# A two-layer encoder on one core: a weight sum made by an accumulating DMA instead of VectorE, with its subtraction moved one product later, and an operand difference made in two parts

## The chip, the cores and the metric

The kernel runs on one core of a Trainium2 chip. A core has TensorE (PE, matrix products; PEld is its loading of weights), VectorE (DVE), ScalarE (ACT), GpSimd (POOL) and SyncE (SP). SP issues the plain loads; GpSimd issues the transfers that add to what lies at their destination. The metric is the device time of one execution in microseconds.

## The reference

The reference is an encoder trunk in float32 with 528 tokens (512 and 16 learned ones), width 1024, two layers. Each layer is a half feed-forward network (FFN), a mixer, and a second half FFN:

```python
def swiglu(x, w_gate, w_up, w_down):
    return (jax.nn.silu(x @ w_gate) * (x @ w_up)) @ w_down

for l in range(DEPTH):
    h = h + 0.5 * swiglu(rmsnorm(h, norm_gains[l, 0]),
                         ffn_w_gate[l, 0], ffn_w_up[l, 0], ffn_w_down[l, 0])
    h = h + mixer(rmsnorm(h, norm_gains[l, 1]), w_in[l], ...)
    h = h + 0.5 * swiglu(rmsnorm(h, norm_gains[l, 2]),
                         ffn_w_gate[l, 1], ffn_w_up[l, 1], ffn_w_down[l, 1])
return rmsnorm(h, final_norm)[:, N_META:]
```

The mixer (gated linear attention beside softmax attention) is not touched by the change. The inner width of an FFN is 2816, that is 22 tiles of 128 columns.

## The kernel before

**Split weights.** Every float32 product is made of three matmuls in the faster type fp32r. `Weights.make` splits each weight block of 128 x 1024 (512 KB) into a high half `whi` (a copy by ScalarE, L287) and a low half `wlo` (block minus high half, VectorE, L288). It works up to four blocks ahead of TensorE's use (`AHEAD_MADE`, one less inside an FFN), and `Weights.fetch` has SP load blocks up to nine ahead. Pools of 3 raw blocks, 4 high and 4 low halves and 3 + 3 sums (tags `wsa`, `wsb`) set when a buffer comes free.

**Seven products in place of eight.** The gate and up projections take their columns in 11 pairs of tiles per FFN. A pair's block product is done by a Winograd scheme with seven products, named by the characters "1" to "7". "1", "2" and "4" use the loaded blocks 11, 12 and 22 as they are. The four others need sums of blocks, for pairs 2 to 10:

- "7" uses s3 = block 21 - block 11. Block 21 is loaded into its buffer (`begin_sums`), and VectorE subtracts in place (L244).
- "6" uses s2 = block 22 + s3, added in place by VectorE (L253).
- "3" uses s4 = s2 - block 12 (VectorE, L256).
- "5" uses s1 = block 21 + block 22: a load, and then an accumulating DMA (`first_sum`, `Weights.add`, L208) which GpSimd issues.

`sums` is called by `make` behind the low half of "1", "2" and "6". Pairs 0 and 1 of each FFN, and the weights of the down-projection, make their sums in other ways, which the change leaves alone.

**Groups.** The 11 pairs form groups of 4, 4 and 3. Behind each of the first two, a fast down-projection follows, again with seven products: an "O" step makes its operands in high and low halves from the four hidden tiles of a quarter (first three of the four, later the last one), and "S" steps run its products on the two halves of the output. The operand "6" is the difference of two quarters (`difference`, L674), then a high half by ScalarE (L669) and a low half by VectorE (L670). In the order of a group's end, `ffn_steps` puts the first products of the next group's first pair (pairs 4 and 8) between the last "S" steps:

```python
turns = [("S", g, *t, 3) for t in zip(AB, "16273465734")]
steps += turns[:6]
for s, c in zip(turns[6:], "1265"):
    steps += [s, ("P", p + 1, c)]
steps.append(turns[-1])
```

So at pairs 4 and 8 there is one "S" step of 24 matmuls between products "2" and "6". At the other pairs "7", "4" and "3" lie in between, of the pair itself or of the one before.

**The order of work.** Each engine runs its instructions in the order in which the program issues them. TensorE writes its sums into PSUM; ScalarE and VectorE take them out (L598 copies a snapshot, L604 adds to it; L716 adds a result of the down-projection to h). ScalarE's copies of weights (L287) and VectorE's low halves (L288) stand in line with these.

Of the kernel before, what the change touches and what calls it, by code (L numbers as in the profile page):

```python
# [14 lines left out]
ALU = mybir.AluOpType  # L15
# [155 lines left out]
class Weights:  # L171
# [59 lines left out]
    def sums(self, f, i, product, w):  # L231


        got, V = self.summed, self.nc.vector
        if (f, i) in OPENING and product in "12":
            (self.begin_sums if product == "1" else self.first_sum)(f, i, *[w] * (product == "1"))
        if i < 2:
            if product == "2":
                s4 = self.negative(f, i, "s4", w)
                self.add(s4, got[f, i, "6"])  # L240
                got[f, i, "3"] = s4
        elif product == "1":
            if i < NPAIR:
                V.tensor_tensor(got[f, i, "7"], got[f, i, "7"], w, ALU.subtract)  # L244
            else:
                got[f, i, "7"] = self.negative(f, i, "s3", w)
                self.add(got[f, i, "7"], self.dram(f, i, "21"))
            if not i < NPAIR:
                self.add(got[f, i, "6"], got[f, i, "7"])
        elif product == "2":  # L250
            self.kept = w
            if i < NPAIR:
                V.tensor_tensor(got[f, i, "6"], got[f, i, "6"], got[f, i, "7"], ALU.add)  # L253
        elif product == "6":
            s4 = self.long.tile([P, SLAB], F32, tag="wsa", name=f"s4_{f[0]}{f[1]}_{i}")
            V.tensor_tensor(s4, w, self.kept, ALU.subtract)  # L256
            got[f, i, "3"] = s4
# [42 lines left out]
    def next(self, name):  # L300
        t = PLAN[self.pos]
        assert t[1] == name, (t, name)
        s, c = divmod(COLUMN[self.pos], SLAB)
        self.pos += 1
        hi, lo = self.use(self.at[s])
        return hi[:, c : c + t[5]], lo[:, c : c + t[5]]
# [18 lines left out]
def build(tc, ctx, xt, wts, win, par, w2, const, umask, out):  # L325
    nc = tc.nc
    V, S, G, TE = nc.vector, nc.scalar, nc.gpsimd, nc.tensor
# [24 lines left out]
    def close_pools(pools):  # L352
        for n in reversed(pools):
            slots.pop(n).release()
# [28 lines left out]
    def h(c, cs=None):  # L383
        return hall[:, c, cs or slice(0, live[0])]
# [184 lines left out]
    def ffn(l, f, norm, done, following):  # L569

        x, rs, up, n = norm.x, None, None, live[0]
        w = n // 2
        pools = open_pools("left", psum=("s2",), c=4, s2=2)
        made, hid, sums, raw, sets = {}, {}, {}, {}, {}
        risen = iter(range(KC))

# [81 lines left out]
        def operand(g, c, ks=slice(0, 4)):  # L658

            src = raw[g][{"1": 0, "2": 2, "5": 0, "6": 0, "7": 1, "3": 3, "4": 2}[c]]  # L660
            if (g, c) not in sets:
                tag = "c" if c in "56" else "g"
                sets[g, c] = [quarter(tag, F32R) for _ in range(2)]
            hi, lo = [t[:, ks] for t in sets[g, c]]
            if c == "3":
                S.activation(hi, src[:, ks], AF.Copy, scale=-1.0)
                V.scalar_tensor_tensor(lo, src[:, ks], -1.0, hi.bitcast(F32), ALU.mult, ALU.subtract)
            else:
                S.copy(hi, src[:, ks])  # L669
                V.tensor_tensor(lo, src[:, ks], hi.bitcast(F32), ALU.subtract)  # L670

        def difference(g, into, a, b, ks=slice(0, 4)):
            r = raw[g]
            V.tensor_tensor(r[into][:, ks], r[a][:, ks], r[b][:, ks], ALU.subtract)  # L674

        def operands_of(g, ks, order):
            for c in order:
                if c == "5":
                    difference(g, 0, 1, 0, ks)
                operand(g, c, ks)  # L680
# [10 lines left out]
        def fast_down(g, dq, c, part):  # L691
            last = sum(GROUPS[: g + 1]) - 1
            kinds = ("ss", "s2") if last % 2 == 0 else ("s2", "ss")
            st = made.setdefault(("S", g, dq), {})
            where = {"2": "Y", "5": "Z", "3": "Z"}.get(c, "X")
            begin = c in "125"
            if part != 2:
                if begin:
                    st[where] = pair(kinds[{"Y": 0, "Z": 1, "X": dq}[where]] == "s2")
                st["w"] = st.get("w", {})  # L700
                st["w"][c] = W.op((l, f), NPAIR + QUADS * g + dq, c, ahead=AHEAD_MADE - 1)
            acc = st[where][:, :, :w]
            hi, lo = st["w"][c]
            xs = sets[g, c]
            for k in {1: range(3), 2: range(3, 4), 3: range(4)}[part]:
                for j in range(2):
                    for i, (a, b) in enumerate(((hi, 0), (hi, 1), (lo, 0))):
                        TE.matmul(acc[:, j], a[:, j, k], xs[b][:, k], start=bool(begin and k == 0 and i == 0),  # L708
                                  stop=k == 3 and i == 2, skip_group_check=not begin)
            if part == 1:  # L710
                return
            st["w"].pop(c)
            for m, q in {"1": [(0, 0)], "2": [(0, 0)], "5": [(1, 1)], "6": [(0, 1)], "3": [(0, 1)], "7": [(1, 1)],
                         "4": [(1, 0)]}[c]:
                to = hall[:, 4 * dq + m : 4 * dq + m + 3 : 2, q * w : (q + 1) * w]
                V.tensor_tensor(to, to, acc, ALU.add)  # L716
            if dq == 1:
                sets.pop((g, c))
            operands_behind(g, dq, c)

        def down(g, m, first, last):
            base = 2 * sum(GROUPS[:g])
            other = (sum(GROUPS[: g + 1]) - 1) % 2 == 0
            kind = "s2" if other == (m // 2 % 2 == 1) else "ss"
            width = 2 * GROUPS[g]
            if g == len(GROUPS) - 1 and m >= LATE and done is None:
                sums[m] = Acc("ss" if m == LATE else "s2", cut=True), [W.next("ffn_w_down") for _ in range(width)]
                if m == KC - 1:
                    ending([sums[c] for c in range(LATE, KC)], [hid[base + k] for k in range(width)], rs)
                return  # L730
            if first == 0:
                sums[m] = Acc(kind)
            product("ffn_w_down", sums[m], [hid[base + k] for k in range(first, last)], last - first,
                    begin=first == 0, end=last == width)
            if last < width:
                return
            add_to_h(m, sums[m])
            if g == len(GROUPS) - 1:
                lower_h(m, rs)
                (done or finish_chunk)(m)  # L740
# [3 lines left out]
        for i, step in enumerate(steps):  # L744
            if step[0] == "P":
                if step[1:] == (0, "5") and norm.acc is None:
                    for c in range(KC):
                        norm.square(c)
                product_of_pair(*step[1:])
                if step[1:] == (0, "5"):  # L750
                    rs, up = norm.rs(True)
                    W.behind = prev_act[0]
                if step[1] in (2, 3) and step[2] in "6574":
                    m = next(risen)
                    V.scalar_tensor_tensor(h(m), h(m), -1.0, up, ALU.mult, ALU.mult)
                if i == last_op:
                    close_pools(norm.pools)
                    following()
            elif step[0] == "S":
                fast_down(*step[1:])  # L760
            elif step[0] == "O":
                g, last = step[1:]
                operands_of(g, slice(3, 4) if last else slice(0, 3), "215" if last else "125")
                if last:
                    difference(g, 0, 3, 0)
                    operand(g, "6")
            else:
                down(*step[1:])
# [444 lines left out]
    def finish_chunk(c):  # L1213
        fin.square(c)
        gain(c, slice(0, SEQ))

    def ending(sums, operand, rs):

        table("abs_reciprocal_sqrt_and_small")
# [64 lines left out]
    for l in range(DEPTH):  # L1284
        a, b, c = norms[3 * l : 3 * l + 3]
        ffn(l, 0, a, b.chunk, lambda: operand_pools(b, "x"))
        close_pools(bp.pop())
        mixer(l, b, c.chunk_of_pair, lambda: (operand_pools(c, "xc"), bp.append(block_pools())))
        if l < DEPTH - 1:
            d = norms[3 * l + 3]  # L1290
            ffn(l, 1, c, d.pair_of, lambda: operand_pools(d, "xc"))
        else:
            ffn(l, 1, c, None, lambda: None)
# [72 lines left out]
```

## Time and profile before

| | before |
|---|---|
| median of 3 runs | 2219.3 us (2217.36 to 2219.31) |
| profiled execution | 2218.53 us |
| its span | 2216.8 us |
| granted TensorE clock | 0.998 |
| TensorE busy | 2164.6 us (98%) |
| VectorE busy | 1784.4 us (80%) |
| ScalarE busy | 1210.7 us (55%) |
| GpSimd busy | 101.5 us (5%) |
| queue of GpSimd's DMAs (q0) | 60.82 MB, 15.6% of the 16 DMA engines' span |
| queue of SP's DMAs (q1) | 245.53 MB, 33.0% |

The times come from one execution that the hardware profiler recorded. In the lines of its views `out<-in` names the tiles without their numbers: `whi<-w` is the high half of a loaded or summed weight block, `wlo<-w,whi` its low half, `s` a sum, `g` and `c` operands and hidden tiles, `ss` a PSUM sum. A timeline line has the start, the duration, the engine, the source line and the operation; in brackets stands the idle time before it and what ended it. A wait line has the engine and line that waited, what for, the total in us, how many times and the longest. A DMA line has the issues, the size of each and the median from issue to landing.

### The profile page before, as it was taken

The numbers are of one execution on the slowest core, as the hardware profiler recorded it, in microseconds if no ns is written. First come the engines' busy times: TensorE is split into PE (matmuls) and PEld (weight loads), VectorE is DVE, ScalarE is ACT, GpSimd is POOL, SyncE is SP. The second block draws the span as 40 slices with busy tenths as digits, with TensorE's granted clock in tenths as the row PEclk, the third lists the DMA queues.
The fourth block names the chain that finished last, engine by engine and source line by source line (L and its number), as shares of the span: only waits on it lengthen the run. The fifth ranks groups of instructions, "written<-read, shape, count | busy, mean of one in ns | idle before, by whom it ended". The sixth has DMA issues, their size and how long they took to land.

```text
span 2216.8 us, 40090 instructions
## 1 busy us (share of the span) xinstructions
PE 2164.6 (98%) x16506; PEld 2070.7 (93%) x16506; DVE 1784.4 (80%) x2695; ACT 1210.7 (55%) x1779; POOL 101.5 (5%) x120
## 2 busy tenths in 40 slices
PE   7999999999999999999999999999999999999998
PEld 6899999989999999999999999999788888999997
DVE  7887978486886688888789879775879767997987
ACT  7444545354785555454575445553557836554543
POOL 1000000000000001000010000000000001000100
PEclk9999999999999999999999999999999999999999
DMA  9675753212113467666566757432121146776752
GB/s 278 172 199 165 190 158 101 86 48 67 48 39 118 116 168 200 190 184 187 158 162 187 207 159 194 143 110 77 48 82 53 42 135 153 196 200 180 191 161 67
DMA packets 87463, 311.41 MB, mean 140 GB/s; under 512 B 9712, under 2 KB 12144, under 8 KB 87280
## 3 DMA queue, kind: packets, MB, share of 16 engines
q1 hardware_dynamic: 68624, 245.53, 33.0%
q0 software_dynamic: 16704, 60.82, 15.6%
q8 instruction: 130, 2.13, 0.4%
q10 hardware_dynamic: 1952, 2.50, 0.3%
q14 instruction: 53, 0.43, 0.1%
HBM read 289.94 MB, written 2.10 MB: 132 GB/s over the span
## 4 chain that ended last, share of the span: by engine, by line
PE 79%; DVE 11%; ACT 3%; issue 2%; DMA 1%; DVEq 0%; POOL 0%; ACTq 0%; POOLq 0%
PE ss L594 36%; PE mm L461 13%; PE ss L708 11%; PE ss L461 10%; PE sm L461 2%; DVE wlo L288 2%; DVE g L674 1%; PE sm L1069 1%; PE ss L1044 1%; DVE h L716 1%; PE ss L467 1%; DMA w<-win 1%; PE sm L1085 1%; ACT t L440 1%; DVE c L670 1%
## 5 line engine op out<-in xcount | busy, mean ns | idle before, releaser
L594 PE MATMUL ss<-xc,whi 128*128 128x264 f32 (+1 forms) x4928 | 905.3, 285 | 15.6 <-ACT whi L287 7.6
L594 PEld LDWEIGHTS ss<-xc,whi 128*128 128x128 f32 x4928 | 765.3, 189 | 20.5 <-ACT c L598 8.4
L594 PE MATMUL ss<-xc,wlo 128*128 128x264 f32 (+1 forms) x2464 | 701.5, 285 | 8.8 <-DVE wlo L288 8.7
L594 PEld LDWEIGHTS ss<-xc,wlo 128*128 128x128 f32 x2464 | 465.4, 189 | 11.2 <-DVE wlo L288 11.0
L288 DVE TENSOR_TENSOR wlo<-w,whi 128x1024 fp32r<-128x1024 f32 (+1 forms) x337 | 408.0, 1217 | 64.1 <-ACT whi L287 63.9
L287 ACT CAST whi<-w 128x1024 fp32r<-128x1024 f32 (+1 forms) x337 | 349.4, 1048 | 175.2 <-PE ss L594 82.1
L461 PE MATMUL mm<-x,whi 128*128 128x264 f32 (+1 forms) x1712 | 384.8, 315 | 0.0
L461 PEld LDWEIGHTS mm<-x,whi 128*128 128x128 f32 x1712 | 278.4, 188 | 16.6 <-issue 1.0
L461 PE MATMUL mm<-x,wlo 128*128 128x264 f32 (+1 forms) x856 | 266.0, 315 | 0.0
L708 PE MATMUL ss<-g,whi 128*128 128x264 f32 (+1 forms) x1280 | 238.6, 285 | 1.5 <-ACT g L669 1.4
L287 ACT CAST whi<-raw 128x1024 fp32r<-128x1024 f32 x126 | 132.1, 1048 | 163.6 <-PE mm L461 102.8
L598 ACT COPY c<-ss 128x528 f32<-128x528 f32 (+1 forms) x132 | 78.4, 594 | 259.1 <-PE ss L594 259.1
L288 DVE TENSOR_TENSOR wlo<-raw,whi 128x1024 fp32r<-128x1024 f32 x126 | 153.9, 1221 | 59.2 <-ACT whi L287 58.4
L708 PEld LDWEIGHTS ss<-g,whi 128*128 128x128 f32 x1280 | 199.0, 189 | 2.1 <-ACT g L669 1.6
L708 PE MATMUL ss<-g,wlo 128*128 128x264 f32 (+1 forms) x640 | 181.7, 284 | 0.0
L461 PEld LDWEIGHTS mm<-x,wlo 128*128 128x128 f32 x856 | 159.5, 188 | 8.5 <-issue 0.7
L461 PE MATMUL ss<-g,whi 128*128 128x264 f32 (+2 forms) x900 | 166.2, 299 | 0.0
L461 PEld LDWEIGHTS ss<-g,whi 128*128 128x128 f32 x900 | 131.7, 188 | 5.3
L208 POOL DMA_DIRECT2D w<-win x60 | 52.8, 880 | 1580.1 <-DVE wlo L288 463.9
L708 PEld LDWEIGHTS ss<-g,wlo 128*128 128x128 f32 x640 | 120.9, 189 | 0.0
L440 ACT ACTIVATE c<-c 128x528 f32<-128x528 f32 (+1 forms) x88 | 56.5, 642 | 93.6 <-DVE c L638 89.3
L708 PE MATMUL ss<-c,whi 128*128 128x264 f32 (+1 forms) x512 | 100.3, 289 | 7.1 <-DVE c L670 6.6
(267 smaller groups left out, 3375.3 us busy)
## 6 DMA issues: line engine op xcount, KB each, us to landing
w<-win SPq DMA_DIRECT2D x335, 512.0 KB, 4.5
raw<-wts SPq DMA_DIRECT2D x126, 512.0 KB, 3.3
w<-win POOLq DMA_DIRECT2D x60, 512.0 KB, 7.5
s<-win POOLq DMA_DIRECT2D x24, 512.0 KB, 7.0
w<-s POOLq DMA_DIRECT2D x24, 512.0 KB, 5.6
s<-w POOLq DMA_DIRECT2D x8, 512.0 KB, 7.7
h<-xt SPq DMA_DIRECT2D x3, 528.0 KB, 7.1
out<-h ACTq DMA_DIRECT2D x4, 256.0 KB, 2.4
```

The source lines that it names most:

```text
L208: self.nc.gpsimd.dma_start(t, src, accum_op=ALU.add)
L287: nc.scalar.copy(hi[:, cs], w[:, cs])
L288: nc.vector.tensor_tensor(lo[:, cs], w[:, cs], hi[:, cs].bitcast(F32), ALU.subtract)
L440: prev_act[0] = S.activation(*args, **kw).ins
L461: TE.matmul(acc.half[i][:width], lhs, rhs[:, acc.spans[i]], start=first, stop=last)
L467: TE.matmul(a, weights, x[:, hs], start=True, stop=True)
L594: TE.matmul(acc[:, j], a[:, j, k], b[:, at], start=bool(begin and k == 0 and i == 0), stop=k == len(x) - 1 and i == 2, skip_group_check=no ...
L598: W.behind = S.copy(part(st, q), acc).ins
L670: V.tensor_tensor(lo, src[:, ks], hi.bitcast(F32), ALU.subtract)
L674: V.tensor_tensor(r[into][:, ks], r[a][:, ks], r[b][:, ks], ALU.subtract)
L708: TE.matmul(acc[:, j], a[:, j, k], xs[b][:, k], start=bool(begin and k == 0 and i == 0), stop=k == 3 and i == 2, skip_group_check=not begin)
L716: V.tensor_tensor(to, to, acc, ALU.add)
```

## The change

It has two parts. In `sums` the subtraction for s3 is no longer done at product "1": the raw block is kept, and VectorE subtracts it at product "2", where it added s2 before. s2 is then made by an accumulating DMA from s3's buffer to s2's, issued by GpSimd. It concerns nine pairs in each of four FFNs, 36 sums. At pairs 4 and 8 this DMA is issued behind the one of `first_sum` of the same pair.

In `ffn` the difference for operand "6" is done in both "O" steps, three quarters of the columns in the first and one quarter in the last, rather than whole in the last. There are eight such sites, two in each FFN.

```diff
@@ -241,7 +241,7 @@
         elif product == "1":
             if i < NPAIR:
-                V.tensor_tensor(got[f, i, "7"], got[f, i, "7"], w, ALU.subtract)
+                self.kept1 = w
             else:
@@ -250,7 +250,8 @@
         elif product == "2":
             self.kept = w
             if i < NPAIR:
-                V.tensor_tensor(got[f, i, "6"], got[f, i, "6"], got[f, i, "7"], ALU.add)
+                V.tensor_tensor(got[f, i, "7"], got[f, i, "7"], self.kept1, ALU.subtract)
+                self.add(got[f, i, "6"], got[f, i, "7"])
@@ -760,9 +761,10 @@
             elif step[0] == "O":
                 g, last = step[1:]
-                operands_of(g, slice(3, 4) if last else slice(0, 3), "215" if last else "125")
+                ks = slice(3, 4) if last else slice(0, 3)
+                operands_of(g, ks, "215" if last else "125")
+                difference(g, 0, 3, 0, ks)
                 if last:
-                    difference(g, 0, 3, 0)
                     operand(g, "6")
```

In the changed order of VectorE's instructions the subtraction of the pairs 4 and 8 stands where the addition L253 stood; at the other pairs it keeps its place.

## The prediction

> **What bounds the kernel now.** I began with the page: the busy table, then the chain that ended last.
>
> ```profile
> span 2216.8 us, 40090 instructions
> PE 2164.6 (98%) x16506; PEld 2070.7 (93%) x16506; DVE 1784.4 (80%) x2695; ACT 1210.7 (55%) x1779; POOL 101.5 (5%) x120
> PE 79%; DVE 11%; ACT 3%; issue 2%; DMA 1%; DVEq 0%; POOL 0%; ACTq 0%; POOLq 0%
> ```
>
> TensorE is busy for 2164.6 of 2216.8 us. All that is not matmul is 52 us, so the change can only move time by closing a pause of TensorE or by opening one. VectorE is 80% busy; work taken from it counts only where TensorE waits for it. So I read next the waits of TensorE.
>
> ```profile
> PE ss L594 <- DVE wlo L288: 8.7, 8, 3.1
> PE ss L594 <- ACT whi L287: 7.6, 2, 7.4
> PE ss L708 <- DVE c L670: 6.6, 8, 0.9
> PE ss L594 <- ACT c L598: 6.1, 11, 0.7
> ```
>
> The third line is the one the change aims at: eight waits, 6.6 us, all for the low half of operand "6" of the fast down-projection, which is made behind the difference. No line names the weight sum L253 or the difference L674 directly, and the two lines on the weight halves have ten waits together. TensorE thus seldom waits for weights, and a weight sum that comes too late would show as a new wait.
>
> **Part 1: the early difference (a gain).** One site, from the timelines of VectorE, ScalarE and TensorE at the end of group 1 of the first FFN:
>
> ```profile
> 249.48 1.25 DVE L674 TENSOR_TENSOR g<-g,g 128x1056 f32<-128x1056 f32 x1
> 250.65 1.31 DVE L716 TENSOR_TENSOR h<-h,ss 128x528 f32<-128x528 f32 x2
> 251.93 1.26 DVE L670 TENSOR_TENSOR c<-g,c 128x1056 fp32r<-128x1056 f32 x1
> 250.82 1.07 ACT L669 CAST c<-g 128x1056 fp32r<-128x1056 f32 x1 [1.03 <-DVE g L674]
> 253.24 0.39 PE L708 MATMUL ss<-c,whi 128*128 128x264 f32 x1 [0.91 <-DVE c L670]
> ```
>
> The chain is difference 1.25, ScalarE's copy 1.07, the low half 1.26, and TensorE pauses 0.91 us for it. The change does three quarters of that difference at the first "O" step, so here a piece of 128x264 remains. The pieces that are in the trace already give its time:
>
> ```profile
> 244.37 0.77 DVE L648 TENSOR_TENSOR g<-c 128x264 f32<-128x264 f32 x2
> 245.27 0.43 DVE L670 TENSOR_TENSOR g<-g,g 128x264 fp32r<-128x264 f32 x1
> L674 DVE TENSOR_TENSOR g<-g,g 128x792 f32<-128x792 f32 x6 | 5.9, 983 | 0.2
> ```
>
> 0.43 for 1.25 takes 0.82 us from the chain. ScalarE stood idle for 1.03 us before its copy, so the copy moves up by all of the 0.82. VectorE has two additions, L716, between; if what they add is ready earlier they move up too and the low half starts 0.8 us earlier; if not, the low half stays where it is and nothing is won. So the bounds are 0 and 0.82 per site, and in all no more than the 6.6 us of the wait row. The two additions start without a pause before them, so I take nearly all of it: seven sites of 0.75 and about 0.3 for the shorter first one, 5.5 us.
>
> What the early part adds: eight differences of 128x792 (0.98 us each by the row above) in the first "O" step, ahead of the low halves of the next weights. Those are made about four products ahead of TensorE; I take 0. Were that cover gone it would cost up to 8 x 0.98 = 7.8 us, but the 10 waits for weights above say that it is not gone anywhere but at the start.
>
> **Part 2: the removed additions.** Seen from the source lines:
>
> ```profile
> L253 DVE TENSOR_TENSOR w<-w,w x36: 1217/1220/1227, 55.6 to 2127.1; 128x1024 f32<-128x1024 f32 x36
> L244 DVE TENSOR_TENSOR w<-w,w x36: 1215/1222/1227, 49.2 to 2125.8; 128x1024 f32<-128x1024 f32 x36
>   DMA w<-win: 33.4, 16
> ```
>
> 36 x 1.22 = 44 us of VectorE vanish, and 36 subtractions go from product "1" to product "2". No wait of TensorE hangs on either, so I take 0; the most that it could give is the 8.7 us of waits for low weight halves. VectorE's idle 33.4 us before L244 belongs to VectorE alone and is not a gain. Keeping the raw block of "1" one product longer holds one of three buffers longer; the loads run several products ahead, so 0 as well.
>
> **Part 3: the accumulating DMA (the cost).** Sum "6" is no longer an addition of 1.22 us but a subtraction, an issue by GpSimd and a transfer to wait for. For the other pairs the halves of "6" are made long after the sum; at pair 9 of the first FFN (VectorE's and ScalarE's timelines) they come 17 us later, more than any transfer below needs:
>
> ```profile
> 284.07 1.22 DVE L253 TENSOR_TENSOR w<-w,w 128x1024 f32<-128x1024 f32 x1
> 301.44 1.05 ACT L287 CAST whi<-w 128x1024 fp32r<-128x1024 f32 x1
> ```
>
> It is tight for the first pairs of groups 1 and 2, pairs 4 and 8, eight sites in all: there product "6" follows "2" with a single step of the down-projection between. Pair 8 of the first FFN, from the timelines:
>
> ```profile
> 269.08 1.22 DVE L244 TENSOR_TENSOR w<-w,w 128x1024 f32<-128x1024 f32 x1
> 271.37 0.88 POOL L208 DMA_DIRECT2D w<-win  x1 [24.81 <-DVE h L716]
> 273.72 1.22 DVE L253 TENSOR_TENSOR w<-w,w 128x1024 f32<-128x1024 f32 x1
> 275.14 1.05 ACT L287 CAST whi<-w 128x1024 fp32r<-128x1024 f32 x1
> 276.42 1.22 DVE L288 TENSOR_TENSOR wlo<-w,whi 128x1024 fp32r<-128x1024 f32 x1
> 282.24 0.40 PE L594 MATMUL ss<-xc,whi 128*128 128x264 f32 x2
> 282.48 0.28 PE L594 MATMUL ss<-xc,wlo 128*128 128x264 f32 x1
> ```
>
> Before, "6" has its halves at 276.2 and 277.6, six and five microseconds ahead of TensorE. In the changed kernel the subtraction stands in L253's place. L244 ahead of it is gone, so it ends between 273.8 (all behind L244 moves up) and 274.9 (nothing moves); I take 273.9 and the issue at 274.0. That is 2.6 us behind the issue of first_sum's transfer at 271.37, on the same queue. With 1.05 for ScalarE, 1.22 for VectorE and about 0.1 between, the low half is ready 2.4 us after landing, so TensorE pauses by whatever the landing exceeds 282.48 - 2.4 = 280.1, a latency of 6.1 us.
>
> What such a transfer takes the trace shows in groups only. First the medians of GpSimd's queue, then three single ones:
>
> ```profile
> w<-win POOLq DMA_DIRECT2D x60, 512.0 KB, 7.5
> w<-s POOLq DMA_DIRECT2D x24, 512.0 KB, 5.6
> s<-w POOLq DMA_DIRECT2D x8, 512.0 KB, 7.7
> ```
>
> ```profile
> 771.47 0.86 POOL L208 DMA_DIRECT2D s<-win  x1 [3.44 <-ACT s L203]
> 773.54 0.89 POOL L208 DMA_DIRECT2D s<-w  x1 [1.20 <-ACT t L505]
> 978.65 0.86 POOL L208 DMA_DIRECT2D w<-win  x1 [3.27 <-DVE g L648]
> 982.51 0.87 POOL L208 DMA_DIRECT2D w<-s  x1 [3.00 <-DMA s<-win]
> ```
>
> The DMA view of the window at 773 us gives the second of these a landing after 7.2 us (2.07 behind its forerunner), that at 982 us gives the fourth 4.7 us (3.86 behind):
>
> ```profile
> s<-w POOLq DMA_DIRECT2D x1, 512.0 KB, 7.2
> w<-s POOLq DMA_DIRECT2D x1, 512.0 KB, 4.7
> ```
>
> So the closer behind another accumulation, the longer. The new one is 2.6 behind, nearer to the 7.2 us; and the DMA engines are loaded at this place, as the windows table shows (the last two columns are DMA share and GB/s):
>
> ```profile
> 275.30:279.00 3.70, 3.70 (x33) 3.70 (x32) 3.70 (x4) 1.95 (x2) 0.00 (x0) 1.00 0.95 248
> ```
>
> From 275.3 to 279.0, the very time in which the transfer would run, they are 95% busy. I take 7.2: landing 281.2, a pause of 1.1 us. At 4.7 or 5.6 there is none; at 7.7 from the late issue (275.0) it is 2.6.
>
> One site is tighter, pair 4 of the last FFN:
>
> ```profile
> 1981.30 1.22 DVE L253 TENSOR_TENSOR w<-w,w 128x1024 f32<-128x1024 f32 x1
> 1989.37 0.40 PE L594 MATMUL ss<-xc,whi 128*128 128x256 f32 x2
> 1989.60 0.28 PE L594 MATMUL ss<-xc,wlo 128*128 128x256 f32 x1
> ```
>
> Issue at about 1982.6, landing by 1989.8, low half 1992.2: a pause of 2.6 us. The eight sites together cost 7 x 1.1 + 2.6 = 10.3 us; I add about 1 us for the start of the first FFN, where weights already come late (the wait of up to 3.1 us above). Bounds: 0, and 7 x 2.6 + 3.1 = 21 us.
>
> Queued behind the waiting ScalarE and VectorE instructions are the next weight copy, an addition L716 and the low half of the next down-projection weight. They become some 5 us late, to about 284 us, and TensorE wants them after product "6", from 285.2 on; I count nothing more. On GpSimd nothing of weight stands behind the new issue, 0.87 us each.
>
> The Trainium skill, page "DMA: Bandwidth & Descriptors", section "Anatomy of one DMA — SWDGE (gpsimd) path", states for a transfer that GpSimd issues a fixed part of about 2 us plus the bytes over 436 GB/s. For 512 KB that is an estimate of 3.2 us, with which all eight pauses would vanish and the sum would be the gain alone. The trace disagrees: its medians for this size are 5.6 to 7.7 us, so I go by the rows.
>
> **Sum.** -5.5 + 10.3 + 1 = +5.8 us. The profiled execution took 2218.53 us with its span of 2216.8, so it would come to 2224.3; the median of the runs, 2219.3, lies 0.8 above it, so 2225 us.
>
> **The rivals.** Forecast: the transfer queues behind first_sum's and TensorE pauses some 1.3 us at eight places, 2225 us; chance 0.55.
>
> (a) The transfer lands in 4.5 to 6 us, as the w<-s group's median of 5.6 says (it too is a sum in SBUF). No site pauses, only the early difference counts: 2219.3 - 5.5 = 2214, with the full 6.6 us 2212.7. It decides below 6.1 us from issue to landing. For it: that median. Against: most of those have no forerunner within 3 us, and the 95% above. Chance 0.14. The estimate from the Trainium skill's page above leads to this rival too.
>
> (b) Gain and cost cancel: with 6.8 us the pause is 0.7 at seven sites and 2.2 at the eighth, 7.1 us against 5.5, or the gain is the smaller part and the pauses are few. Between 2215 and 2223; chance 0.21. That the change does nothing at all lies here too, at 2219.
>
> (c) Heavier queueing: the two transfers share the loaded engines, each slows the other and SP's loads. With 7.7 from the late issue it is 21 - 5.5 = +15.5, 2235. Chance 0.10.
>
> **How the numbers follow.** What a measurement of this kernel can tell from no change is about 0.2%, 4.4 us. Faster by more than that is (a) alone where it keeps most of the gain: 0.13. Within it: (b) and a remainder of (a): 0.22. Slower: the forecast and (c): 0.65. The range 2213 to 2235 takes in (a) at its likely end and (c); what is left out is one in ten at either side.
>
> **What would show it.** In the changed kernel's profile: TensorE's wait row L708 <- DVE L670 falls from 6.6 to about 1 us; L594 <- L288 (or L287) grows by 8 to 12 us with waits at pairs 4 and 8 alone; the issues table has 36 transfers w<-w on GpSimd's queue; those at pairs 4 and 8 take 7 us or more. VectorE's busy time falls by some 44 us. I am wrong if those transfers take under 6.1 us (then faster), or if L708's wait stays, or if TensorE waits at the other pairs as well.

## The result, and the profile after

The changed kernel takes 2271.1 us (median of 5 runs, 2266.83 to 2272.49) against 2219.31 us; the ratio is 1.0227, 95% interval 1.0216 to 1.0239. It is 52 us slower. Forecast were 6 us slower and at most 16: the sign was right, the size was not, and the time lies far outside the range.

The page of the changed kernel, the span, the busy times, the software queue's line and the chain:

```profile
span 2269.2 us, 40136 instructions
PE 2181.6 (96%) x16506; PEld 2083.7 (92%) x16506; DVE 1742.4 (77%) x2667; ACT 1211.9 (53%) x1779; POOL 133.5 (6%) x156
q0 software_dynamic: 21888, 79.70, 19.8%
PE 66%; DVE 16%; DMA 9%; ACT 5%; issue 4%; POOL 0%; SPq 0%; DVEq 0%; POOLq 0%; ACTq 0%
```

Two numbers grew by amounts that add to the loss. Time without a matmul went from 52.2 to 87.6 us, that is 35.4 more. But TensorE's busy time grew as well, by 17.0 us for the same 16506 matmuls: they ran slower. VectorE is 42 us less busy, as foreseen, and nothing was gained by it. DMA is now 9% of the chain instead of 1%.

TensorE's waits, the lines that answer to the four of before:

```profile
PE ss L595 <- ACT whi L288: 31.8, 9, 7.5
PE ss L595 <- DVE wlo L289: 23.5, 26, 3.5
PE ss L595 <- ACT c L599: 6.1, 11, 0.7
PE ss L709 <- DVE c L671: 4.0, 9, 0.7
```

The waits for high weight halves grew by 24.2 us, those for low halves by 14.8; the wait for operand "6" fell by 2.6. Together +36.4, which is about all of the idle time that was added.

Pair 8 of the first FFN, from the timelines of GpSimd, VectorE, ScalarE and TensorE:

```profile
276.76 0.86 POOL L208 DMA_DIRECT2D w<-win  x1 [25.31 <-DVE h L717]
279.27 0.89 POOL L208 DMA_DIRECT2D w<-w  x1 [1.65 <-DVE w L253]
277.64 1.22 DVE L253 TENSOR_TENSOR w<-w,w 128x1024 f32<-128x1024 f32 x1
288.76 1.04 ACT L288 CAST whi<-w 128x1024 fp32r<-128x1024 f32 x1 [8.63 <-DMA w<-w]
289.83 1.23 DVE L289 TENSOR_TENSOR wlo<-w,whi 128x1024 fp32r<-128x1024 f32 x1 [7.66 <-ACT whi L288]
289.85 0.51 PE L595 MATMUL ss<-xc,whi 128*128 128x264 f32 x2 [2.58 <-ACT whi L288]
291.11 0.43 PE L595 MATMUL ss<-xc,wlo 128*128 128x264 f32 x1 [0.75 <-DVE wlo L289]
```

The DMA view gives the new transfer 9.4 us from issue to landing:

```profile
w<-w POOLq DMA_DIRECT2D x1, 512.0 KB, 9.4
```

The order of events is the one foreseen: subtraction, issue 2.5 us behind first_sum's, landing, high half, low half, a pause of 2.58 + 0.75 us. At the eight sites the latency was 8.9 to 11.3 us and the pause 2.8 to 5.2 us, 30.4 us in all.

Now the windows of the same place. A line has start:end, the length, the busy times of TensorE, its weight loads, VectorE, ScalarE and GpSimd with the number of instructions, then granted clock, DMA share and GB/s:

```profile
284.00:287.00 3.00, 3.00 (x27) 3.00 (x26) 0.00 (x0) 0.00 (x0) 0.00 (x0) 1.00 1.05 255
287.00:290.00 3.00, 0.42 (x4) 0.21 (x3) 0.17 (x1) 1.24 (x2) 0.00 (x0) 1.00 0.29 107
290.00:293.00 3.00, 2.25 (x11) 2.04 (x12) 3.00 (x4) 1.70 (x2) 0.00 (x0) 0.72 0.00 0
293.00:296.00 3.00, 3.00 (x20) 3.00 (x19) 3.00 (x4) 0.37 (x1) 0.00 (x0) 0.71 0.34 89
296.00:299.00 3.00, 3.00 (x27) 3.00 (x26) 2.62 (x3) 2.69 (x4) 1.51 (x2) 1.00 0.91 300
```

Behind the pause the granted clock falls, and in the window from 293 to 296, where TensorE has no gap, it does 20 matmuls instead of 27. That is the busy time that grew. By the clock's records half speed followed seven of the eight pauses, for 3.4 or 6.8 us each and 30.6 us in all; the shortest pause, 2.77 us at pair 4 of the second FFN, is the one without it. One more stretch of 6.8 us lies in the start of the first FFN, behind a pause of 3.55 us; the kernel before has a single stretch of 3.4 us, at 120.8 us (each without the very end of the program). Half of 30.6 + 6.8 - 3.4 us is the 17.0 us.

The last two columns show a second thing: DMA goes from 1.05 to 0.00 between 290 and 293 us and is back at 0.91 from 296 on. SP's loads had stopped, and then bunched. The waits of SP's queue between 284 and 294 us say what for:

```profile
SPq L198 <- DVE wlo L289: 9.8, 1, 9.8
SPq L198 <- DMA w<-win: 2.4, 1, 2.4
```

A landing held it for 2.4 us, but then it stood 9.8 us for a raw block that VectorE still had to read for a low half; and VectorE, which works in order, was standing at the late low half of product "6". At the eight sites this wait is 9.3 to 11.7 us; before it was 4.2 to 5.4 us at the same places.

What a bunch can do is seen one pair later, at pairs 5 and 6 of the second FFN (VectorE's and TensorE's timelines, and the DMA view for the load issued at 934.38):

```profile
944.99 1.22 DVE L253 TENSOR_TENSOR w<-w,w 128x1024 f32<-128x1024 f32 x1 [7.89 <-DMA w<-win]
946.14 1.22 DVE L289 TENSOR_TENSOR wlo<-w,whi 128x1024 fp32r<-128x1024 f32 x1
947.41 0.39 PE L595 MATMUL ss<-xc,wlo 128*128 128x264 f32 x1 [1.99 <-DVE wlo L289]
w<-win SPq DMA_DIRECT2D x1, 512.0 KB, 10.5
```

A load of SP (median 4.5 us before) takes 10.5 us. The subtraction waits for it 7.89 us, and the low half of another block, ready to be made, stands behind the subtraction on VectorE. In all, VectorE's idle time ahead of these subtractions grew from 33.4 us (before) to 87.1 us:

```profile
  DMA w<-win: 87.1, 17
```

### The profile page after: what moved, and what is told of

It is laid out like the page before. It is cut to its first block, busy times and chain, and to the rows that moved or that the text cites. A ratio compares the mean times of both kernels' runs of the same rounds, so it can differ in the third digit from the quotient of the medians.

```text
span 2269.2 us, 40136 instructions
## 1 busy us (share of the span) xinstructions
PE 2181.6 (96%) x16506; PEld 2083.7 (92%) x16506; DVE 1742.4 (77%) x2667; ACT 1211.9 (53%) x1779; POOL 133.5 (6%) x156
## 3 DMA queue, kind: packets, MB, share of 16 engines
q1 hardware_dynamic: 68624, 245.53, 32.3%
## 4 chain that ended last, share of the span: by engine, by line
PE 66%; DVE 16%; DMA 9%; ACT 5%; issue 4%; POOL 0%; SPq 0%; DVEq 0%; POOLq 0%; ACTq 0%
PE ss L595 29%; PE mm L462 12%; PE ss L462 10%; PE ss L709 6%; DMA w<-win 6%; DVE wlo L289 5%; DMA w<-w 3%; PE sm L462 2%; ACT whi L288 2%; PE sm L1071 1%; DVE g L675 1%; PE ss L1046 1%; DVE g L671 1%; DVE h L717 1%; PE ss L468 1%
## 5 line engine op out<-in xcount | busy, mean ns | idle before, releaser
L595 PE MATMUL ss<-xc,whi 128*128 128x264 f32 (+1 forms) x4928 | 918.5, 287 | 40.6 <-ACT whi L288 31.8
L595 PEld LDWEIGHTS ss<-xc,whi 128*128 128x128 f32 x4928 | 775.6, 191 | 47.2 <-ACT whi L288 34.9
L595 PE MATMUL ss<-xc,wlo 128*128 128x264 f32 (+1 forms) x2464 | 709.9, 288 | 23.7 <-DVE wlo L289 23.5
L595 PEld LDWEIGHTS ss<-xc,wlo 128*128 128x128 f32 x2464 | 471.7, 191 | 30.0 <-DVE wlo L289 29.8
L709 PEld LDWEIGHTS ss<-g,wlo 128*128 128x128 f32 x640 | 120.8, 189 | 0.0
L253 DVE TENSOR_TENSOR w<-w,w 128x1024 f32<-128x1024 f32 x36 | 44.0, 1222 | 87.1 <-DMA w<-win 87.1
```

The source lines that it names most:

```text
L253: V.tensor_tensor(got[f, i, "7"], got[f, i, "7"], self.kept1, ALU.subtract)
L595: TE.matmul(acc[:, j], a[:, j, k], b[:, at], start=bool(begin and k == 0 and i == 0), stop=k == len(x) - 1 and i == 2, skip_group_check=no ...
```

## The experiments

All times are medians; the kernel before came to 2219.3 to 2221.1 us beside them. "Idle" is the span less TensorE's busy time in the profiled run.

| run | us | ratio, 95% interval | idle | TensorE busy |
|---|---|---|---|---|
| before | 2219.3 | | 52.2 | 2164.6 |
| the change | 2271.1 | 1.0227 (1.0216 to 1.0239) | 87.6 | 2181.6 |
| early_only | 2215.3 | 0.998 (0.9971 to 0.9989) | 48.5 | 2162.2 |
| later_vector | 2215.4 | 0.9978 (0.9969 to 0.9987) | 47.7 | 2166.0 |
| vector_at_4_8 | 2213.6 | 0.9976 (0.9966 to 0.9986) | 47.7 | 2162.0 |
| dma_at_4_8 | 2272.3 | 1.0236 (1.0222 to 1.025) | 86.2 | 2187.0 |
| s1_behind | 2269.5 | 1.0223 (1.0205 to 1.0242) | 82.1 | 2182.3 |
| half_dma | 2259.3 | 1.0168 (1.0154 to 1.0182) | 74.8 | 2184.4 |
| s1_vector | 2259.9 | 1.0171 (1.0156 to 1.0186) | 72.2 | 2180.5 |
| dma_at_1 | 2228.8 | 1.0034 (1.0021 to 1.0047) | 59.5 | 2167.4 |
| dma_at_1_first | 2219.8 | 0.9998 (0.9989 to 1.0007) | 52.6 | 2164.8 |
| late_hi_8 | 2284.6 | 1.0289 (1.0275 to 1.0303) | 92.0 | 2192.0 |
| late_hi_7 | 2272.8 | 1.0238 (1.0225 to 1.0252) | 84.3 | 2186.2 |
| late_hi_6 | 2265.1 | 1.0204 (1.0188 to 1.0219) | 81.1 | 2183.2 |
| late_hi_5 | 2259.9 | 1.018 (1.0166 to 1.0194) | 77.3 | 2178.3 |
| late_hi_4 | 2251.9 | 1.0135 (1.0119 to 1.0152) | 72.7 | 2178.6 |

### Which part loses

My theory (A) was that the eight accumulating DMAs at pairs 4 and 8 make the whole loss. The rivals: the kept raw block holds up loads (B), or all 36 transfers load the DMA engines (C). Four kernels split the change.

early_only has the second part of the change's diff alone.

> Only the early difference; all weight sums as before. Every theory expects the pause of TensorE for the low half of operand 6 to shrink from 0.9 to 0.1-0.4 us at seven of the eight sites: 3 to 5.5 us below before, 2214 to 2216 us. If the difference in the first O step held something up, it would come out at before's 2219 or above.

later_vector:

```diff
                 V.tensor_tensor(got[f, i, "7"], got[f, i, "7"], self.kept1, ALU.subtract)
-                self.add(got[f, i, "6"], got[f, i, "7"])
+                V.tensor_tensor(got[f, i, "6"], got[f, i, "6"], got[f, i, "7"], ALU.add)
```

> The change, but all 36 second sums are added by VectorE behind the late subtraction; no new DMA. Theory A (the accumulating DMAs of pairs 4 and 8 make the loss): the loss is gone, within 2 us of the early difference alone, 2213 to 2218 us. Theory B (keeping the raw block of product 1 holds up SP's loads, and these make TensorE wait): most of the loss stays, above 2240 us.

vector_at_4_8:

```diff
-                self.add(got[f, i, "6"], got[f, i, "7"])
+                if i in (4, 8):
+                    V.tensor_tensor(got[f, i, "6"], got[f, i, "6"], got[f, i, "7"], ALU.add)
+                else:
+                    self.add(got[f, i, "6"], got[f, i, "7"])
```

> The change, with VectorE's addition at pairs 4 and 8 only; the other 28 sums keep the accumulating DMA. Theory A: the eight pauses of 3 to 5 us and the half-speed clock behind them are gone, 2213 to 2221 us. Theory C (all 36 transfers load the DMA engines and make loads late): only the eight pauses themselves, 30 us, go, and the waits at pairs 5, 6, 9 and 10 stay: 2230 to 2240 us.

dma_at_4_8, on the kernel before:

```diff
         elif product == "1":
-                V.tensor_tensor(got[f, i, "7"], got[f, i, "7"], w, ALU.subtract)
+                if i in (4, 8):
+                    self.kept1 = w
+                else:
+                    V.tensor_tensor(got[f, i, "7"], got[f, i, "7"], w, ALU.subtract)
         elif product == "2":
-                V.tensor_tensor(got[f, i, "6"], got[f, i, "6"], got[f, i, "7"], ALU.add)
+                if i in (4, 8):
+                    V.tensor_tensor(got[f, i, "7"], got[f, i, "7"], self.kept1, ALU.subtract)
+                    self.add(got[f, i, "6"], got[f, i, "7"])
+                else:
+                    V.tensor_tensor(got[f, i, "6"], got[f, i, "6"], got[f, i, "7"], ALU.add)
```

> The kernel before, with late subtraction and accumulating DMA at pairs 4 and 8 alone and no early difference. Theory A: nearly all of the loss, 2219 + 30 us of pauses + 17 us of half-speed clock + some 5 us in the pairs behind = 2265 to 2275 us, at least as slow as the whole change. Theory C: only the pauses and the clock, 2255 to 2262 us. Theory B: under 2240 us, since 28 of 36 raw blocks are no longer kept.

A holds, B and C fall. The eight transfers alone give 2272.3 us. Without them the change is 0.2% faster than before, with 28 accumulating DMAs or with none. The early difference does what was said; the wait row of early_only for operand "6":

```profile
PE ss L708 <- DVE c L670: 3.0, 7, 0.5
```

3.0 us instead of 6.6. These three kernels beat both; their intervals overlap, so none is the best of them.

### Is it the pause or the DMA that slows the clock?

late_hi_8, on the kernel before, has no new DMA (the others of the series have 7, 6, 5 and 4 for 8):

```diff
+                late = not isinstance(load, int) and load[1] in (4, 8) and load[2] == "6"
-                    nc.scalar.copy(hi[:, cs], w[:, cs])
+                    for _ in range(1 + 8 * late):
+                        nc.scalar.copy(hi[:, cs], w[:, cs])
```

> The kernel before, with no DMA added: ScalarE writes the high half of the weight of product 6 nine times instead of once at pairs 4 and 8, 8 x 1.05 = 8.4 us later than the 5 to 6 us of slack. TensorE should pause by 3.4 us at eight places (2.3 for the high half, 1.1 for the low), 27 us in all. If the half-speed clock follows from the pause itself, 1.5 to 3.5 us come on top at each, and the time is 2258 to 2275 us; if it is a matter of the DMA traffic, 2245 to 2250.

> As before, with eight copies: pauses of 3.0 us, 24 us in all. Clock at full speed: 2244 us. Clock halved behind each pause, as the trace of the change has it: 2260 to 2270 us.

> As before, with seven copies: pauses of 1.95 us, 16 us in all. With the clock at full speed 2235 to 2238 us; if the clock already falls at all eight sites as behind longer pauses, 2 to 3.5 us more at each, 2252 to 2264; if it falls at some of them, in between.

> The kernel before, with six copies for the high half of product 6 at pairs 4 and 8 instead of nine (each 1.05 us). With nine TensorE paused 3.6 + 0.45 us at each site; three fewer leave 0.9. A pause this short should leave the clock at full speed: 8 x 0.9 = 7 us, 2226 to 2229 us. If any pause halves the clock, 2240 or more.

> The kernel before, with five copies for the high half of product 6 at pairs 4 and 8. With six to nine copies the pauses at these sites came to 2.3, 2.5, 3.5 and 4.4 us; one copy fewer than six should leave about 1.2 us, below every pause behind which the clock was seen to fall (1.5 us and more): 8 x 1.2 = 10 us, clock as before, 2228 to 2232 us. If ScalarE's delay costs more than the pause, above 2240.

The windows of late_hi_8 behind pair 8's pause, columns as above:

```profile
294.00:298.00 4.00, 0.45 (x4) 0.24 (x3) 2.18 (x3) 3.90 (x4) 0.00 (x0) 1.00 0.00 0
298.00:301.00 3.00, 2.47 (x9) 2.16 (x10) 2.94 (x3) 0.03 (x1) 0.00 (x0) 0.51 0.00 0
301.00:304.00 3.00, 3.00 (x16) 3.00 (x15) 1.69 (x2) 0.00 (x0) 0.00 (x0) 0.50 0.47 141
304.00:307.00 3.00, 3.00 (x23) 3.00 (x23) 0.83 (x1) 2.41 (x3) 0.88 (x1) 0.85 0.87 294
```

The clock is at 0.50 for 6.8 us, with no transfer added: the pause does it. TensorE's busy time is 27.4 us up. The stop and the bunch of loads (DMA share 0.00, then 0.87) come here too: SP's queue stands 10.8 us for a low half of VectorE at pair 8. So they belong to any product that is late, and not to the new DMA alone.

All five came out slower than the ranges that were written down for them: late_hi_8 by some 10 us, late_hi_7 and late_hi_6 by 1 to 3, and late_hi_5 and late_hi_4 by 30 and 20 us, where the second outcome (2240 us or more) came instead. For late_hi_4 it was 2251.9 us where 2228 to 2232 stood. TensorE's timeline of late_hi_4 has at pair 8 one pause of 2.92 us for a low half, where 1.2 was meant. VectorE's timeline says why: the low half of "6" now stands behind the next pair's subtraction and addition.

```profile
291.44 0.39 PE L596 MATMUL ss<-xc,wlo 128*128 128x264 f32 x1 [2.92 <-DVE wlo L290]
```

```profile
287.76 1.23 DVE L244 TENSOR_TENSOR w<-w,w 128x1024 f32<-128x1024 f32 x1 [2.20 <-DMA w<-win]
289.02 1.23 DVE L253 TENSOR_TENSOR w<-w,w 128x1024 f32<-128x1024 f32 x1
290.16 1.22 DVE L290 TENSOR_TENSOR wlo<-w,whi 128x1024 fp32r<-128x1024 f32 x1
```

So this series gives no clean price of a pause at full clock. It serves in another way: over the FFN stages of 16 traces, from 90 us on, I counted the pauses of over 0.8 us (those less than 3 us apart added up), and looked at the starts of the matmuls in the 9 us behind. A run of matmuls at half speed followed in 1 of 81 pauses under 1.5 us, in 30 of 58 between 1.5 and 2.8, and in all 45 above. The first 90 us have two exceptions above 2.8: behind 3.13 us in the kernel before (at 64.3 us) and behind 3.38 us in vector_at_4_8 (at 64.0 us) the clock stayed up. No trace here shows a pause of over 3.4 us between two matmuls behind which it stayed up.

### Is the transfer late by the queue, by its bytes, or by the load?

s1_behind:

```diff
-        self.add(s1, self.dram(f, i, "22"))
+        if i not in (4, 8):
+            self.add(s1, self.dram(f, i, "22"))
...
-                self.add(got[f, i, "6"], got[f, i, "7"])
+                second = self.add(got[f, i, "6"], got[f, i, "7"])
+                if i in (4, 8):
+                    with self.tc.issue_after(second.ins):
+                        self.add(got[f, i, "5"], self.dram(f, i, "22"))
```

> The change, but at pairs 4 and 8 GpSimd issues first_sum's accumulation behind the one for sum 6 rather than ahead of it. Theory Q (the transfer is late because it runs behind first_sum's on one queue): it lands 6 to 7 us after its issue, as at the other pairs, rather than 9 to 11; the pauses shrink from 3.3-5.2 to 0.2-1.3 us, too short for the half-speed clock, 2216 to 2226 us. Theory L (the DMA engines are loaded with SP's loads there, whatever the order): it still takes 9 us and more, and the time stays above 2255.

half_dma:

```diff
-                self.add(got[f, i, "6"], got[f, i, "7"])
+                if i in (4, 8):
+                    a, b = [[t[:, cs] for t in (got[f, i, "6"], got[f, i, "7"])]
+                            for cs in (slice(0, SLAB // 2), slice(SLAB // 2, SLAB))]
+                    self.add(*b)
+                    V.tensor_tensor(a[0], a[0], a[1], ALU.add)
+                else:
+                    self.add(got[f, i, "6"], got[f, i, "7"])
```

> The change, but at pairs 4 and 8 VectorE adds one half of the columns (0.6 us) and the accumulating DMA, issued first, the other half (256 KB). Theory Q: it still queues behind first_sum's landing, but its own share halves, from 4-6 us to 2-3 behind that landing; pauses of 1 to 2 us. If the half-speed clock comes only with a pause beyond some 2 us, the time falls to 2225 to 2235; if it comes with any new pause, 2240 to 2250. If the latency is fixed and not by bytes, it stays above 2260.

s1_vector:

```diff
-        self.add(s1, self.dram(f, i, "22"))
+        if i not in (4, 8):
+            self.add(s1, self.dram(f, i, "22"))
...
+                if i in (4, 8):
+                    V.tensor_tensor(got[f, i, "5"], got[f, i, "5"], got[f, i, "6"], ALU.add)
                 V.tensor_tensor(got[f, i, "7"], got[f, i, "7"], self.kept1, ALU.subtract)
                 self.add(got[f, i, "6"], got[f, i, "7"])
```

> The change, but at pairs 4 and 8 sum 5 is added by VectorE (block 21 + block 22, ahead of sum 6), so that GpSimd's queue has only the one accumulating DMA there. If all of the loss comes from two accumulations running together with SP's loads, the transfer lands 6 to 7 us after its issue, pauses stay at 0.3 to 1.2 us, no loads bunch up behind, and the time is 2214 to 2224 us. If the bunching at pairs 5 and 9 comes from the transfer for sum 6 alone (it holds its two buffers and SP waits in order), pauses of 2 to 3 us with a slow clock stay there, above 2250 us as with first_sum's transfer moved behind.

In s1_behind theory Q is right about the latency: ahead of first_sum's transfer the new one lands after 6.2 to 7.0 us at all eight sites. The DMA view and TensorE's timeline at pair 8:

```profile
w<-w POOLq DMA_DIRECT2D x1, 512.0 KB, 6.3
```

```profile
284.51 0.39 PE L600 MATMUL ss<-xc,wlo 128*128 128x264 f32 x1 [0.71 <-DVE wlo L294]
308.48 0.59 PE L600 MATMUL ss<-xc,wlo 128*128 128x264 f32 x1 [3.21 <-DVE wlo L294]
```

The pause at pair 8 is 0.71 us and the clock stays up. Yet the time is 2269.5: a pause of 3.21 us comes one pair later (2.4 to 4.4 us behind each of the eight sites), and the clock falls behind six of the eight. The loss moved. VectorE's timeline gives the reason, the same as in the changed kernel but stronger:

```profile
306.06 1.22 DVE L255 TENSOR_TENSOR w<-w,w 128x1024 f32<-128x1024 f32 x1 [7.81 <-DMA w<-win]
```

SP issues its loads in order, and a load waits until its buffer is free: until a transfer that used it has landed, or until VectorE has read it. In s1_behind the landing is what holds SP: 7.6 to 8.6 us at each of the eight sites, for first_sum's accumulation, which now lands last. (In the change the wait for VectorE's low half is the longer one, as shown above.) The rows name `w<-win`, which first_sum's accumulations and SP's own loads share. The waits of SP's queue for such landings, before, in the change, and in s1_behind:

```profile
SPq L198 <- DMA w<-win: 19.3, 11, 4.5
```

```profile
SPq L198 <- DMA w<-win: 64.3, 19, 6.8
```

```profile
SPq L199 <- DMA w<-win: 107.9, 19, 8.6
```

half_dma took 8.3 us (median of eight) for half the bytes, against 9.7 for the whole in dma_at_4_8, by the DMA views of the two:

```profile
w<-w POOLq DMA_DIRECT2D x8, 256.0 KB, 8.3
```

```profile
w<-w POOLq DMA_DIRECT2D x8, 512.0 KB, 9.7
```

So half of the bytes are worth 1.4 us; the place in the queue is worth more, some 3 us (s1_behind), and 6.2 us and more remain in every order tried at product "2". The time, 2259.3 us, falls between the outcomes that were written down, next to the one for a latency that does not go by bytes (above 2260). The pauses of 1.8 to 2.7 us still pulled the clock down at six of eight sites. In s1_vector nothing else accumulates there, and the transfer takes 7.1 to 8.0 us (7.7 at pair 8, between two loads of SP); VectorE's extra addition of 1.2 us also delays its issue. Pauses of 2.4 to 3.3 us remain at the eight sites, half speed follows at seven of them, and the long pauses at the pairs behind are gone (one of 1.2 us is the largest). Of the two outcomes written down the first missed, and the second had the time right (above 2250 us) but the pauses at the wrong pairs. So the transfer is late without another accumulation beside it, too; how much of each pause is the added addition's, no run separates. The kernel is some 11 us faster than the change, which is what its meeting with first_sum's costs if that addition is free.

### The same transfers at product "1"

dma_at_1 does subtraction and `self.add` at product "1"; dma_at_1_first does that for pairs 4 and 8 alone and keeps VectorE's additions elsewhere, both with the early difference.

```diff
         elif product == "1":
-                self.kept1 = w
+                V.tensor_tensor(got[f, i, "7"], got[f, i, "7"], w, ALU.subtract)
+                self.add(got[f, i, "6"], got[f, i, "7"])
         elif product == "2":
-                V.tensor_tensor(got[f, i, "7"], got[f, i, "7"], self.kept1, ALU.subtract)
-                self.add(got[f, i, "6"], got[f, i, "7"])
```

> The change, but subtraction and accumulating DMA both already at product 1, for all 36 pairs; at pairs 4 and 8 that is about 3.5 us earlier and ahead of first_sum's transfer. All theories expect the landing before it is needed and no pause: 2212 to 2217 us, as the versions with VectorE's addition. If the transfer took over 10 us here too, there would be pauses of 1 us and more, 2222 or above.

> Early difference, and at pairs 4 and 8 alone subtraction and accumulating DMA at product 1; the other 28 sums added by VectorE. With all 36 at product 1 the time was 13 us above the versions with VectorE's addition at pairs 4 and 8, with waits at the pairs behind them. Theory D (back to back with first_sum's, the transfer keeps buffers and the loads of pairs 5 and 9 bunch up behind it): the waits stay though only eight transfers are left, 2220 to 2230 us. Theory E (they need the transfers of pairs 5, 6, 9 and 10 as well): gone, 2213 to 2217 us.

At pair 8 of dma_at_1 the transfer is issued at 268.77 and takes 7.5 us; there is no pause at pairs 4 and 8. But 2228.8 us missed the expectation: pauses of 0.5 to 2.3 us stand at the pairs behind. With eight transfers alone it is 2219.8, 4 us above early_only: most of D's waits are gone, not all. So both theories hold a part, and the 9 us between the two kernels were not taken apart further. That the transfers of the other pairs add to the waits behind is thus likely, but not shown.

## Why the prediction was wrong, point by point

- **What bounds the kernel:** right. Everything that was lost is TensorE idle or slow.
- **Part 1, the early difference, -5.5 us:** right in kind; early_only gives 2.4 to 6.4 us by its interval, its wait row 3.6 (it falls to 3.0 us, and to 4.0 in the change, where about 1 was said).
- **Part 2, 36 additions less, 0 us:** right. vector_at_4_8 takes 28 of them away and gains nothing that its interval shows.
- **Part 3, other pairs, 0 us:** right for the transfers by themselves: the 28 cost nothing in vector_at_4_8. In the change 3.0 us of pauses do stand near pairs 2 and 3 of the last two FFNs, where single transfers took 10.9 and 11.1 us.
- **Part 3, the eight sites, +10.3 us, bound 21:** this is the step that failed, in three ways. First, the latency: 7.2 us was taken from a transfer 2.07 us behind another, and it was 8.9 to 11.3. The engines' share does not tell the two places apart: it was 1.00 and more while the transfer of 7.2 us ran (773.5 to 780.7 us, before), and 0.94 and 0.85 in the two halves of the one at pair 8. What differs is that at pair 8 two loads of SP run beside it for most of its time (issued at 278.89 and 281.41, they took 7.7 and 8.0 us); that these make it slower is argued, not shown. The formula around it (landing + 2.4 us against TensorE's need) held: 3.33 us of pause at pair 8, where it gives 288.7 + 2.4 - 287.5 = 3.6 (the low half was due at 289.85 - 2.58 + 0.24 = 287.5). The pauses came to 30.4 us instead of 10.3.
- Second, **a pause was priced as its own length.** The clock behind it had no term. It is the 17.0 us of busy time, 15.3 us of it behind seven of the eight pauses. The trace of before held the warning, in a window behind pauses of 2.0 us at the end of the first group:

```profile
118.00:121.00 3.00, 1.51 (x10) 1.09 (x9) 2.80 (x6) 1.20 (x3) 0.86 (x1) 0.97 0.65 160
121.00:124.00 3.00, 3.00 (x16) 3.00 (x15) 3.00 (x5) 2.41 (x4) 0.87 (x1) 0.50 1.01 239
```

- Third, **"I count nothing more" for what is queued behind.** I followed ScalarE, VectorE and GpSimd, but not SP's queue. VectorE stands at the late half, so it frees the raw blocks late; SP's loads wait for them and then bunch, and a load in the bunch lands late. The pauses at the pairs behind come to 7.2 us. With the 30.4 at the eight sites, the 3.0 near pairs 2 and 3, the gain of 2.6, and 2.4 us less at the start and the first group's end, they make up about the 35.4 us of idle time. TensorE's waits at other pairs than 4 and 8 were among the signs of being wrong, and they came.
- **The start of the first FFN, +1 us:** its idle time fell by 0.4 us instead, but the half speed behind its pause of 3.55 us cost 3.4 us, which the pause of 3.13 us before had not.
- **The rivals:** (c), heavier queueing, was the right direction with 15.5 us; it named the engines' load and slower loads of SP, but neither the clock nor the stop of SP's queue. (a) is refuted: no transfer at these sites landed below 6.1 us; the quickest took 6.2 us, in s1_behind. The estimate of 3.2 us from the Trainium skill's page "DMA: Bandwidth & Descriptors", section "Anatomy of one DMA — SWDGE (gpsimd) path", is thus half of the least that was measured there.

## What to carry to other kernels

A pause of TensorE is not paid once: when it exceeds some 1.5 us, reckon with the slow clock behind it (it followed about half of the pauses up to 2.8 us and nearly all above), and with the loads that its lateness holds up. Before a sum goes from an engine to an accumulating DMA, look for the place where the result is needed soonest, and take the latency from a transfer that shares queue and load with it; leave the engine's addition there (here eight of 36 sums). Follow a late result through every in-order queue that waits for it or for the buffers behind it, the load queue too.

## What the runs showed of the hardware

**The clock.** Behind such pauses the matmuls ran at half speed (granted clock 0.50). By the clock's records of the 16 traces such a stretch lasted 3.4 us (67 times) or 6.8 us (33 times), the very end of the program left out. The Trainium skill, page "TensorE: Matmul & The Clock Gate", section "Part 1: The HAM clock gate (the "warmup" mystery)", tells of half speed after an idle window of about 3.4 us that runs free of the program. The half speed agrees, and stretches of once and twice that length fit such windows. The length of pause that it takes does not agree: here pauses well short of 3.4 us did it, 30 of 58 between 1.5 and 2.8 us and nearly all above.

**Accumulating DMAs.** On the page of before, q0 has 60.82 MB at 15.6% of the engines' span, q1 245.53 MB at 33.0%: 0.26% against 0.13% for a MB. A transfer that adds at its destination occupied the 16 DMA engines for 1.9 times as long per byte as a load, 2.98 us for 512 KB (15.6% of 2216.8 us over 116 transfers); with 36 more of them it is 2.96 us.
